# All operand tiles lie 144 bytes further, and the third and fourth unit of a block change places

## The chip, the cores and the metric

The kernel runs on one core of a Trainium2 chip. The metric is the device time of one execution in microseconds (us). A run of the kernel is repeated; the time given is the median of the runs.

## The reference

One inference step of a decoder trunk with one layer: a prompt of 256 tokens and 8 x 4 sample tokens, model width 2048, feed-forward width 5632, everything in float32. Around every sub-layer stands an RMS norm.

```python
x = x + 0.5 * rmsnorm(swiglu(rmsnorm(x, g[0]), ffn1_w_in, ffn1_w_out), g[1])
m, sg, sh = hybrid_mixer(rmsnorm(x, g[2]), mix_w_in, ..., mix_w_out, s_gla, s_hgrn)
x = x + rmsnorm(m, g[3])
x = x + 0.5 * rmsnorm(swiglu(rmsnorm(x, g[4]), ffn2_w_in, ffn2_w_out), g[5])
```

`swiglu(x)` is `(silu(x @ w_gate) * (x @ w_up)) @ w_out`. The mixer projects with one large weight, runs two gated linear recurrences on the heads (returning their states), and projects back. All inputs go through the same matrix products: 288 tokens (256 + 32) against every weight.

## The kernel before

**Products in three parts.** Tokens lie along the free dimension (T = 288), features along the partitions. A float32 operand is split into a high and a low part (`fp32r`), and a product is made of three: high x high, high x low, low x high. The normalised activations are split into the tile `xhl`, the hidden layer into `hid`, and each weight tile, loaded by SyncE into one of three `raw` buffers, into `wh`: ACT writes the high part (line 137), then DVE the low part (line 138). A weight tile is a *unit*: two k-tiles of 128 rows by 512 columns. `wh` has four buffers in the pool `hlp`, and two spare ones on the right of the memory (`hx`) around the borders between the sub-layers.

**Blocks.** `block` (line 626) makes 512 output columns: for each unit, for each of four pieces `f` of 128 columns, `two` issues six matmuls (line 647). They take a pair of k-tiles, odd and even, in the order

```python
six = [(0, 1, oh), (0, 1, ol), (0, 0, eh), (1, 1, oh), (0, 0, el), (1, 0, eh)]
```

where the first two numbers pick the weight part (0 high, 1 low; 1 odd, 0 even) and the third the moving part (o odd, e even; h high, l low). So a unit is 24 matmuls of the form 128x288. Blocks of the projections (`gate`, `up`, and those of the mixer and its output, `mo`) have 16 k-tiles, that is eight units. `out` blocks have two units, since each of the eleven 512-wide chunks of the hidden layer is multiplied as soon as it is there; four `out` blocks belong to a chunk, and the last two chunks are taken together (four units to a block). Some units are walked k by k instead (`byk`, lines 636 to 638).

The order of work per feed-forward is gate 0, up 0, gate 1, up 1, out 0, gate 2, up 2, out 1, and so on.

**Where a unit's operands lie.** A *line* is 16 bytes of each partition (`LINE = 4` floats). The start lines of all operands follow a plan:
- `tiles` (line 51) lays out `xhl` and `hid`: one line of lead, then odd high, even high (4 lines further modulo 16), odd low and even low (both 10 lines further modulo 16). Inside each part, four units share a block of memory, interleaved by 36 floats (9 lines). `PART` says which of the four places a unit takes. `xhl` begins at line 3476 and `hid` at line 9204; with the lead line both are at 5 modulo 16.
- A matmul reads its 288 moving columns in turns (`turns_of`): 4 floats (one line) from each of 8 places that are 36 lines apart, then the next line of each.
- `pieces` (line 120) lays out `wh`: odd high lies 390 lines (6 modulo 16) behind even high, odd low 129 (1) and even low 261 (5). Even high begins at a number of lines that `AHEAD_LINES` gives for the unit's number modulo 4. The four buffers of `hlp` are all at 8 modulo 16.

With `PART = (0, 3, 1, 2)` and `AHEAD_LINES = (7, 2, 0, 9)` the start lines modulo 16 are

| unit modulo 4 | moving, odd high | weights, even high | weights, odd high |
|---|---|---|---|
| 0 | 5 | 15 | 5 |
| 1 | 0 | 10 | 0 |
| 2 | 14 | 8 | 14 |
| 3 | 7 | 1 | 7 |

So a unit's first weights (odd high) lie at the same line modulo 16 as its first moving part. A unit's *start line* below is that of its odd high moving part. An even chunk of the hidden layer has the units 0 and 1, an odd one 2 and 3.

Of the kernel before, what the change touches and what calls it, by code (L numbers as in the profile page):

```python
# [9 lines left out]
F32 = mybir.dt.float32  # L10
F32R = mybir.dt.float32r
# [5 lines left out]
P = 128  # L17
TP = 256
TS = 32
T = TP + TS  # L20
# [13 lines left out]
LINE = 4  # L34
PLACES = 8
ODD_HIGH, ODD_LOW, EVEN_LOW = 1536 + 6 * LINE, 512 + LINE, 1024 + 5 * LINE
PART = (0, 3, 1, 2)
AHEAD_LINES = (7, 2, 0, 9)


def columns(t):
# [9 lines left out]
def tiles(pool, n, name):  # L51

    q = n // 2 * T
    t = pool.tile([P, LINE + 10 * LINE + 4 * q], F32R, name=name, tag=name, bufs=1)
    hs, ls = [None] * n, [None] * n
    for dst, odd, at in ((hs, 1, 0), (hs, 0, q + 4 * LINE), (ls, 1, 2 * q + 10 * LINE), (ls, 0, 3 * q + 10 * LINE)):
        r = t[:, LINE + at:LINE + at + q].rearrange("p (b g j c) -> p b g j c", g=PLACES, j=4, c=T // PLACES)
        for u in range(n // 2):
            dst[2 * u + odd] = r[:, u // 4, :, PART[u % 4], :]
    return hs, ls  # L60
# [6 lines left out]
def apart(t, step):  # L67

    return bass.AP(t.tensor, t.offset, [list(t.ap[0]), [step, 2], list(t.ap[1])])


class Weights:
# [14 lines left out]
    def add(self, src, k):  # L87
        self.srcs.append(src)
        self.at.append(LINE * AHEAD_LINES[k // 2 % 4])

# [29 lines left out]
    def pieces(self, n):  # L120

        i = self.split
        raw = self.raws.pop(i)
        pool = self.extra if i in self.extra_units else self.hlp
        hl = pool.tile([P, 2112], F32R, name=f"wh{i}", tag="wh")
        at = self.at[i]
        low = hl[:, at + ODD_LOW:at + ODD_LOW + 2 * (EVEN_LOW - ODD_LOW)]
        l = low.rearrange("p (a c) -> p a c", a=2)[:, ::-1, 0:512]
        h = apart(hl[:, at:at + 512], ODD_HIGH)
        self.parts[i] = (h, l)  # L130
        self.split += 1
        raw = raw.rearrange("p (a b) -> p a b", b=512)
        for j in range(n):
            a = slice(0, 2) if n == 1 else slice(2 * j // n, 2 * j // n + 1)
            w = min(512, 1024 // n)
            c = slice(j * w % 512, j * w % 512 + w)
            i1 = self.nc.scalar.activation(h[:, a, c], raw[:, a, c], AF.Copy).ins  # L137
            i2 = self.nc.vector.tensor_tensor(l[:, a, c], raw[:, a, c], h[:, a, c].bitcast(F32), op=ALU.subtract).ins  # L138
            self.recent = i1, i2
            yield i1, i2  # L140
# [27 lines left out]
def trunk_kernel(ctx, tc, x_prompt, x_sample, state_gla, state_hgrn, norm_gains, f1_in, f1_out, f2_in, f2_out,  # L168
# [6 lines left out]
    xpool = ctx.enter_context(tc.tile_pool(name="xpool", bufs=1))  # L175
# [69 lines left out]
    def wider(n):  # L245

        return {i for i in range(n - 44, n + 4) if i // 2 % 3 == (n + 2) // 2 % 3}
# [38 lines left out]
    x = [xpool.tile([P, T], F32, name=f"x{k}") for k in range(KT)]  # L286
    yg = [xpool.tile([P, 4, T], F32, name=f"y{k}") for k in range(4)]
    y = [yg[k // 4][:, k % 4, :] for k in range(KT)]
    xh, xl = tiles(xpool, KT, "xhl")
    rt = xpool.tile([P, T], F32, name="rt")  # L290
    rp = xpool.tile([P, T], F32, name="rp")
# [224 lines left out]
    class PreNorm:  # L516
# [3 lines left out]
        def __init__(self, name, update, ahead, at):  # L520

            self.name, self.update, self.ahead, self.at, self.late = name, update, ahead, at, []
            self.tmps = None
# [25 lines left out]
    class Fill:  # L549
# [3 lines left out]
        def __init__(self, pool, name, gains, gnext, some, ahead):  # L553
            self.gnext, self.name, self.some, self.ahead = gnext, name, some, ahead
            pool.tile([P, 8], F32, name=f"{name}gap")

            both = list(zip(*tiles(pool, 2 * EARLY, f"{name}hl")))
            self.tiles = [both[:EARLY], both[EARLY:]]
            self.gains = pool.tile([P, 32], F32, name=f"{name}g")[:, 0:EARLY]
            V.tensor_tensor(self.gains, gains[:, 0:EARLY], prm[:, gnext * KT:gnext * KT + EARLY], op=ALU.mult)  # L560
# [146 lines left out]
    def ffn(tag, gcol, gnext, pn, before, fill=None):  # L707
# [2 lines left out]
        border = []  # L710
        with ExitStack() as pools:
            fp = pools.enter_context(tc.tile_pool(name=f"ffn{tag}", bufs=2))
            fp.tile([P, 32], F32, name=f"gap_f{tag}", bufs=1)
            hid, final_tiles = {}, []
            hidden = tiles(fp, 8, f"hid{tag}")

            def do_in(c):
# [1007 lines left out]
    class Border:  # L1725


        def __init__(self, n, gains, gnext, some, ahead=0):
            self.pools = ExitStack()
            top = self.pools.enter_context(tc.tile_pool(name=f"top{gnext}", bufs=1, side="right"))  # L1730
            top.tile([P, 88], F32, name=f"gap{gnext}")
            W.begin_extra(self.pools.enter_context(tc.tile_pool(name=f"hx{gnext}", bufs=2, side="right")), wider(n))
            self.fill = Fill(self.pools.enter_context(tc.tile_pool(name=f"fl{gnext}", bufs=1, side="right")),
                             f"fill{gnext}", gains, gnext, some, ahead)

    pn = pre1 = PreNorm("pre1", x_first, FIRST, 11)
    pn.late.append(prm2)
    u, border = ffn(1, lambda k: hg1[:, k:k + 1], 2, pn, first)
    u, border = mixer(PreNorm("pre2", u, UPDATED, 11), border)
    ffn(2, lambda k: hg1[:, KT + k:KT + k + 1], None, PreNorm("pre3", u, UPDATED, 11), border.pools, border.fill)  # L1740


# [39 lines left out]
```

## Time and profile before

| | |
|---|---|
| median of 3 runs | 2148.63 us (2147.24 to 2149.55) |
| the profiled execution | 2147.9 us |
| its span, first to last instruction | 2146.1 us |
| granted TensorE clock | 0.999 |
| feed-forward 1, mixer, feed-forward 2 end at about | 804, 1360, 2146 us |
| read from HBM | 363.75 MB, 175 GB/s over the span |

How to read it. The span is what the trace holds; the run's time has 1.8 us around it. PE is TensorE's matmuls and PEld its weight loads, which overlap them; DVE is VectorE, ACT ScalarE, POOL GpSimd, SP SyncE. Matmuls are pipelined, and one's duration in the profile (some 286 ns) is longer than the time until the next one starts (some 125 ns). The *chain* follows the work that ended last back through the program; asked in order of time it gives the start of a piece, its length, and the number of instructions that were merged into it (`x192`). In a stretch in which TensorE alone sets the pace, a piece of the chain is the time that so many matmuls take, one after the other; the view can be asked for a short stretch, so that a piece is one unit (`x24`).

### The profile page before, as it was taken

Reading aid. Unit: us, or ns where it says so; the run is one execution under the profiler, and the core shown is the slowest. Engines: PE = TensorE matmul, PEld = TensorE weight load, DVE = VectorE, ACT = ScalarE, POOL = GpSimd, SP = SyncE. Lnnn points to the kernel's source line nnn. Section 1 sums busy time; section 2 is a strip of 40 time slices with the busy share of each in tenths; the row PEclk is TensorE's granted clock in tenths of the full one; section 3 lists DMA queues with packets and bytes.
Section 4 is the critical chain, followed back from the end, with each engine's and each line's share of the span. In section 5 each row is a group of like instructions: output and inputs, shape, how many; then the busy total and the mean of one; then the engine's idle time right before and its main releaser. Section 6 shows DMA issues by size and latency. Waiting matters only on the chain.

```text
span 2146.1 us, 43224 instructions
## 1 busy us (share of the span) xinstructions
PE 2134.7 (99%) x17828; PEld 2115.5 (99%) x17828; DVE 1379.6 (64%) x2253; ACT 1016.8 (47%) x1537; POOL 180.5 (8%) x327
## 2 busy tenths in 40 slices
PE   9999999999999999999999999999999999999998
PEld 9999999999999999999999999999999999999998
DVE  7655546655665568888888755854665466556656
ACT  6453433343344445655676654644334333433344
POOL 2000000000000001333110000000000020122005
PEclk9999999999999999999999999999999999999999
DMA  7665555555556654678666664555555565666556
GB/s 222 180 177 176 171 176 176 176 171 177 175 176 188 179 175 139 199 211 221 178 188 183 184 190 145 161 176 176 176 177 172 175 186 177 183 186 186 176 171 163
DMA packets 227334, 384.87 MB, mean 179 GB/s; under 512 B 21362, under 2 KB 60864, under 8 KB 227136
## 3 DMA queue, kind: packets, MB, share of 16 engines
q1 hardware_dynamic: 213872, 365.02, 56.7%
q0 software_dynamic: 10992, 16.77, 3.0%
q8 instruction: 140, 2.29, 0.4%
q10 hardware_dynamic: 2272, 0.31, 0.1%
q14 instruction: 58, 0.48, 0.1%
HBM read 363.75 MB, written 11.80 MB: 175 GB/s over the span
## 4 chain that ended last, share of the span: by engine, by line
PE 93%; DVE 3%; ACT 2%; issue 1%; DMA 1%; POOL 0%; DVEq 0%; ACTq 0%; POOLq 0%
PE gate L647 26%; PE out L647 24%; PE up L647 24%; PE hfq L647 5%; PE mo L647 4%; PE hi L647 2%; PE v L647 2%; ACT wh L137 1%; DVE wh L138 1%; PE gate L637 1%; PE gate L636 0%; PE gate L638 0%; PE os L1401 0%; PE sc L1147 0%; ACT ls L202 0%
## 5 line engine op out<-in xcount | busy, mean ns | idle before, releaser
L138 DVE TENSOR_TENSOR wh<-raw,wh 128x1024 fp32r<-128x1024 f32 (+1 forms) x676 | 821.4, 1216 | 572.2 <-ACT wh L137 571.2
L137 ACT ACTIVATE wh<-raw 128x1024 fp32r<-128x1024 f32 (+1 forms) x676 | 709.9, 1052 | 886.5 <-PE gate L647 275.9
L647 PE MATMUL gate<-xhl,wh 128*128 128x288 f32 x4584 | 588.3, 288 | 1.2 <-DVE u L740 0.8
L647 PEld LDWEIGHTS gate<-xhl,wh 128*128 128x128 f32 x4584 | 582.0, 187 | 2.8 <-issue 0.7
L647 PE MATMUL out<-hid,wh 128*128 128x288 f32 x4224 | 532.5, 286 | 0.0
L647 PEld LDWEIGHTS out<-hid,wh 128*128 128x128 f32 x4224 | 530.2, 187 | 0.1
L647 PE MATMUL up<-xhl,wh 128*128 128x288 f32 x4152 | 527.9, 287 | 0.0
L647 PEld LDWEIGHTS up<-xhl,wh 128*128 128x128 f32 x4152 | 525.3, 187 | 0.0
L831 DVE TENSOR_TENSOR y<-out,y 128x288 f32<-128x288 f32 x287 | 116.8, 451 | 73.2 <-PE out L647 73.1
L647 PE MATMUL hfq<-xhl,wh 128*128 128x288 f32 x768 | 103.3, 290 | 0.0
L647 PEld LDWEIGHTS hfq<-xhl,wh 128*128 128x128 f32 x768 | 98.6, 187 | 0.9
L788 POOL DMA_DIRECT2D xT<-b x64 | 37.2, 587 | 733.2 <-PE gate L647 550.6
L647 PE MATMUL mo<-xhl,wh 128*128 128x288 f32 x768 | 97.6, 288 | 0.2 <-ACT y L1715 0.2
L647 PEld LDWEIGHTS mo<-xhl,wh 128*128 128x128 f32 x768 | 97.1, 187 | 0.5 <-ACT y L1715 0.4
L991 POOL MEMSET ahl<- 128x512 f32 x1 | 0.5, 525 | 782.6 <-PE out L647 782.6
L742 ACT ACTIVATE hid<-u 128x288 fp32r<-128x288 f32 x88 | 37.5, 445 | 59.5 <-DVE u L741 58.0
L740 DVE TENSOR_TENSOR u<-up,rt 128x288 f32<-128x288 f32 x88 | 37.8, 451 | 29.2 <-PE up L647 29.2
L647 PE MATMUL hi<-xhl,wh 128*128 128x288 f32 x384 | 53.5, 291 | 0.0
L735 DVE TENSOR_TENSOR g<-gate,rt 128x288 f32<-128x288 f32 x80 | 33.6, 454 | 30.7 <-PE gate L647 30.7
L647 PEld LDWEIGHTS hi<-xhl,wh 128*128 128x128 f32 x384 | 50.2, 188 | 0.5
L647 PE MATMUL v<-xhl,wh 128*128 128x288 f32 x360 | 49.4, 290 | 0.0
L202 ACT ACTIVATE g<-g 128x288 f32<-128x288 f32 x88 | 36.0, 436 | 25.6 <-DVE g L735 25.2
(409 smaller groups left out, 1525.3 us busy)
## 6 DMA issues: line engine op xcount, KB each, us to landing
raw<-in_ffn_w_in_dram SPq DMA_DIRECT2D x350, 512.0 KB, 3.8
raw<-in_ffn_w_out_dram SPq DMA_DIRECT2D x176, 512.0 KB, 3.7
raw<-in_mix_w_in_dram SPq DMA_DIRECT2D x64, 512.0 KB, 4.4
raw<-in_mix_w_in_dram SPq DMA_DIRECT2D x96, 256.0 KB, 3.4
raw<-in_mix_w_out_dram SPq DMA_DIRECT2D x32, 512.0 KB, 3.8
out_dram<-s POOLq DMA_DIRECT2D x32, 256.0 KB, 3.0
s<-in_state_gla_dram SPq DMA_DIRECT2D x16, 256.0 KB, 6.3
s<-in_state_hgrn_dram SPq DMA_DIRECT2D x16, 256.0 KB, 5.8
```

Of the source, the lines that this page charges most:

```text
L137: i1 = self.nc.scalar.activation(h[:, a, c], raw[:, a, c], AF.Copy).ins
L138: i2 = self.nc.vector.tensor_tensor(l[:, a, c], raw[:, a, c], h[:, a, c].bitcast(F32), op=ALU.subtract).ins
L202: ins = S.activation(out, in_, func, **kw).ins
L637: yield lambda: PE.matmul(dst, w[0][:, a, c], parts[1], start=False, stop=False)
L647: product[0] = PE.matmul(dst, w[low][:, a, c], part, start=k == n == 0, stop=k == nk - 2 and n == 5).ins
L735: V.tensor_tensor(g, ps, rt, op=ALU.mult)
L740: ins = V.tensor_tensor(u, ps, rt, op=ALU.mult).ins
L742: S.activation(hh[f], columns(u), AF.Copy)
L788: queues[n % len(queues)].dma_start(dst[q * TS:(q + 1) * TS, 4 * g:4 * g + 4, :, cols].rearrange("p k t c -> p (k t) c"), b32[rows, q])
L831: V.tensor_tensor(y[k], ps, y[k], op=ALU.add)
L991: G.memset(ahl[:, 512:].bitcast(F32), 0.0)
```

## The change

No instruction is added, removed or moved: on every engine the instructions stand in the same order with the same waits. Addresses alone change.

```diff
-PART = (0, 3, 1, 2)
-AHEAD_LINES = (7, 2, 0, 9)
+PART = (0, 3, 2, 1)
+AHEAD_LINES = (7, 2, 9, 0)
...
 def tiles(pool, n, name):
...
-    t = pool.tile([P, LINE + 10 * LINE + 4 * q], F32R, name=name, tag=name, bufs=1)
+    t = pool.tile([P, 10 * LINE + 4 * q], F32R, name=name, tag=name, bufs=1)
...
-        r = t[:, LINE + at:LINE + at + q].rearrange("p (b g j c) -> p b g j c", g=PLACES, j=4, c=T // PLACES)
+        r = t[:, at:at + q].rearrange("p (b g j c) -> p b g j c", g=PLACES, j=4, c=T // PLACES)
...
-        at = self.at[i]
+        at = LINE + self.at[i]
...
+    xpool.tile([P, 40], F32, name="gap_x")
     xh, xl = tiles(xpool, KT, "xhl")
...
-            fp.tile([P, 32], F32, name=f"gap_f{tag}", bufs=1)
+            fp.tile([P, 40], F32, name=f"gap_f{tag}", bufs=1)
...
-            top.tile([P, 88], F32, name=f"gap{gnext}")
+            top.tile([P, 120], F32, name=f"gap{gnext}")
```

Two things happen.

Everything that TensorE reads in these products moves by 144 bytes, which is nine lines. For `xhl` a gap of 160 bytes stands ahead of the tile and the lead line of 16 bytes is gone. All that is allocated behind it (`raw`, `wh`, the pools of the sub-layers) moves by 128 bytes; inside `wh` one line is put ahead, and `hid` gets 32 more bytes of gap in exchange for its lead line. On the right side of the memory, which is filled from the end, the spare weight buffers and the fill's operands move by 112 bytes the other way (seven lines), which is the same modulo 16 lines. `raw`, read by ACT and DVE alone, moves by 128 bytes.

The third and fourth unit of each four change places, in the moving operand (`PART`) and in the weights (`AHEAD_LINES`) alike. Together the start lines modulo 16 become:

| unit modulo 4 | moving, odd high | weights, even high | weights, odd high |
|---|---|---|---|
| 0 | 14 | 8 | 14 |
| 1 | 9 | 3 | 9 |
| 2 | 0 | 10 | 0 |
| 3 | 7 | 1 | 7 |

The fourth unit stays where it was: nine lines on by the shift, nine back by the exchange.

## The prediction

> **What bounds the kernel now.** I read the page first, for what is full:
>
> ```profile
> span 2146.1 us, 43224 instructions
> PE 2134.7 (99%) x17828; PEld 2115.5 (99%) x17828; DVE 1379.6 (64%) x2253; ACT 1016.8 (47%) x1537; POOL 180.5 (8%) x327
> ...
> PE 93%; DVE 3%; ACT 2%; issue 1%; DMA 1%; POOL 0%; DVEq 0%; ACTq 0%; POOLq 0%
> ```
>
> TensorE is in action for 99% of the span and carries 93% of the chain that ended last. Nobody feeds it late: the longest waits of PE by the waits view are
>
> ```profile
> PE o L1394 <- ACT kd L1502: 1.2, 1, 1.2
> ...
> PE gate L647 <- DVE u L740: 0.8, 2, 0.5
> ```
>
> so the time is the number of matmuls times what one takes. The change adds and removes no instruction; only what one matmul takes can move the time. A busy share of 99% does not tell that, so I read the chain in order of time, where whole blocks stand as one piece:
>
> ```profile
> 302.96 24.21 PE up L647 x192
> 327.17 24.03 PE out L647 x192
> ...
> 399.63 23.98 PE out L647 x192
> ```
>
> 192 matmuls of one form, 128x288, take 24.21 us in an `up` block (126.1 ns each) and 23.98 us in four `out` blocks (124.9 ns). Something in the `up` block costs 0.23 us. The same view, asked for one unit of 24 matmuls at a time, finds where. Units 0 to 3 of this `up` block, then unit 4:
>
> ```profile
> 302.96 2.99 PE up L647 x24
> 305.96 2.99 PE up L647 x24
> 308.95 3.08 PE up L647 x24
> 312.03 3.04 PE up L647 x24
> 315.07 2.99 PE up L647 x24
> ```
>
> The third and fourth unit of each four are slow, by 0.09 and 0.05 us. That could be the lines at which they start (14 and 7), the jump by which they are reached, or merely their number in the block, through what ACT and DVE do beside them. The `out` blocks, of two units each, tell these apart. First an odd chunk, whose units start at lines 14, 7, 14, 7:
>
> ```profile
> 327.17 2.99 PE out L647 x24
> 330.16 3.02 PE out L647 x24
> 333.18 2.99 PE out L647 x24
> 336.17 3.02 PE out L647 x24
> ```
>
> Here a unit at line 14 costs 2.99 us: the line alone isn't slow. Now the last, double chunk, lines 14, 7, 5, 0, 14, 7, from its first unit and from its fifth:
>
> ```profile
> 762.02 2.99 PE out L647 x24
> ...
> 774.01 3.08 PE out L647 x24
> 777.10 3.04 PE out L647 x24
> ```
>
> The same line 14 costs 2.99 us when the unit before it lay at line 7 (762.02) and 3.08 us when it lay at line 0 (774.01, though this is the first unit of its block). So neither the number nor the line decides, but **the pair of a unit and the one before it**. At such a seam TensorE still streams the last product of the old unit, from its even high part (start line + 4), while it already loads the new unit's first weights, which lie at the new unit's own start line modulo 16. I call old line + 4 - new line, modulo 16, the distance of the seam. Inside a unit, from one 128-column piece to the next, it is always 4. An even chunk gives the seams 0 to 5 and 5 to 0:
>
> ```profile
> 399.63 2.99 PE out L647 x24
> 402.62 2.99 PE out L647 x24
> 405.61 3.01 PE out L647 x24
> ```
>
> All seams of the kernel before, with the time of the unit that follows:
> - distance 9 (5 to 0): 2.99 us
> - distance 13 (7 to 14): 2.99 us
> - distance 15 (0 to 5): 3.01 us
> - distance 11 (14 to 7): 3.02 us, and 3.04 us where the unit at 14 was slow itself
> - distance 6: 3.08 us for 0 to 14, but 2.99 us for 7 to 5 (the rows at 302.96 and 315.07)
>
> **The change part by part.**
>
> *All operands 9 lines (144 bytes) further.* Moving parts and weights go together, so within every unit each product meets its weights at the same difference as before. The rows above have units of 2.99 us at the lines 5, 0 and 14, so the lines as such have no price, and I put the common shift at 0 us. What covers it is that both shifts are equal, and that isn't quite so: the two spare weight buffers on the right move 7 lines down, which is the same modulo 16 but not modulo 32. They hold 24 of the 626 units that are walked in this form. If each of these became as slow as the slowest row, that would be 24 x 0.09 = 2.2 us; I take 0, and keep 2.2 for the range.
>
> *Third and fourth unit change places.* The start lines become 14, 9, 0, 7. The seams of a block of eight units were 9, 6, 11, 6; they become 9 (14 to 9), 13 (9 to 0), 13 (0 to 7), 13 (7 to 14). Both distances have rows of 2.99 us for the unit behind them. Four units take now, by the row of 192 at 302.96, 24.21 / 2 = 12.105 us; they will take 4 x 2.99 = 11.96 us: 0.145 us less. In the built program there are 118 places where a unit at line 14 follows one at 0 (112 in the blocks of eight units, 6 in the two double chunks; where a unit is walked k by k, it isn't counted and keeps its time). 118 x 0.145 = 17.1 us.
>
> In the `out` blocks nothing is gained: even chunks go from 5, 0 to 14, 9 with distances 9 and 15 as before; odd chunks from 14, 7 to 0, 7, so that distance 11 (now 7 to 0, 3.02 us) is at the first unit and 13 (0 to 7, 2.99 us) at the second: 0 us.
>
> *What is late next.* Per unit ACT and DVE split one weight tile:
>
> ```profile
> L138 DVE TENSOR_TENSOR wh<-raw,wh 128x1024 fp32r<-128x1024 f32 (+1 forms) x676 | 821.4, 1216 | 572.2 <-ACT wh L137 571.2
> L137 ACT ACTIVATE wh<-raw 128x1024 fp32r<-128x1024 f32 (+1 forms) x676 | 709.9, 1052 | 886.5 <-PE gate L647 275.9
> ```
>
> One after the other they are 1.05 + 1.22 = 2.27 us, below 2.99 us, and run a unit or more ahead. They read `raw`, which moves by 128 bytes, and write parts that move by 144; the profile prices no such shift. The nearest rows are two operations of ACT on one form:
>
> ```profile
> L742 ACT ACTIVATE hid<-u 128x288 fp32r<-128x288 f32 x88 | 37.5, 445 | 59.5 <-DVE u L741 58.0
> ...
> L202 ACT ACTIVATE g<-g 128x288 f32<-128x288 f32 x88 | 36.0, 436 | 25.6 <-DVE g L735 25.2
> ```
>
> They differ by 2%; that much on 2.27 us is 0.05 us either way, inside the 0.7 us that is free. The cover is thin only in the mixer, as two stretches show (columns: PE, PEld, DVE, ACT, POOL, clock, DMA share, GB/s):
>
> ```profile
> 302.96:327.17 24.21, 24.21 (x195) 24.21 (x194) 11.31 (x13) 9.48 (x12) 0.00 (x0) 1.00 0.55 175
> 1100.00:1200.00 100.00, 99.90 (x1121) 96.94 (x1120) 89.43 (x202) 71.37 (x160) 7.58 (x11) 1.00 0.63 181
> ```
>
> DVE is at 11.3 of 24.2 us in the `up` block, but at 89% here. 25 of the 118 places lie in the mixer's projections, worth 3.6 us; I let a third of that be lost to DVE, 1.2 us (between nothing and all of it). The weights come at 175 GB/s and would need 177; the row above shows 181.
>
> **Sum.** 2147.9 us of the profiled execution (span 2146.1, 1.8 us around it) - 17.1 + 1.2 = **2132 us**. The median of the runs, 2148.63, lies 0.7 us higher; I don't add this.
>
> *A rule that speaks against it.* "SBUF — State Buffer" of the Trainium skill, section "Who interferes with whom", says that PE and ACT never wait on anyone, and "TensorE: Matmul & The Clock Gate", section "Step-by-step: what each phase is for", that loading the next weights takes no read bandwidth from the running matmul. By these the place of operands would be worth nothing and the time 2148 us. The trace doesn't agree: the same form on the same line takes 2.99 or 3.08 us per 24.
>
> **The rivals.**
> - *One of the new seams is worse than its distance says.* Distance 6 shows that it doesn't tell all: 7 to 5 is harmless, 0 to 14 isn't. Distance 13 is measured for one pair only, 7 to 14; 9 to 0 and 0 to 7 are carried over. One unit in four left at 3.04 us gives 118 x (0.145 - 0.05) = 11 us, 2137 us; at 3.08 us 118 x (0.145 - 0.09) = 6.5 us, 2141 us. Chance 0.12.
> - *The change does nothing*: the slowness belongs to something that moves along, so that another two of the four units are slow. Then 12.105 us stay and the time is 2148 us. For it: nobody in the trace names what a slow matmul waits for. Against: the four seams of distance 13 in each odd `out` chunk. Chance 0.08, which includes the skill's rule.
> - *Slower: both carried-over seams start a slow stretch.* The unit at 0 and the one at 7 then cost 3.08 us each: 2.99 + 2.99 + 3.08 + 3.08 = 12.14 us, 118 x 0.035 = 4.1 us more; in the odd chunks of `out` a pair goes from 6.01 to 3.02 + 3.08 = 6.10 us, 36 times 0.09 = 3.2 us. Together 2155 us, and 2161 us if the unit at 14 after a slow one still takes 3.04 us (118 x 0.05). It is slower from the point where two of the three new seams are slow. For it: after 0 to 14 the slowness lasts into a second unit, so it can feed itself. Against: distance 6 stood at all slow starts, and vanishes. Chance 0.08.
>
> **How the numbers follow.** The forecast has 0.72, between 2128 us (nothing lost in the mixer, also the 3.01 and 3.02 us of `out` gone, 30 x 0.02 + 36 x 0.03 = 1.7 us, and a run 0.7 us below the profiled one, as the lowest shown is) and 2137 us (all of the mixer's 3.6 us lost and the 2.2 us of the spare buffers paid). With the first rival, up to 2142 us, that is 0.84; a little of it falls outside. Range 2128 to 2143 us. 0.2%, about what a measurement of this kernel can tell from no change, is 4.3 us: faster 0.84, same 0.08, slower 0.08.
>
> **What would show it.** Right: the `up` and `gate` blocks at 23.92 us (8 x 2.99), all their units at 2.99 us, `out` blocks at 23.98 and 24.03 us as now. The step on seams is wrong if a unit of 3.04 us or more remains in the steady blocks; which line it has tells which seam. The step on the common shift is wrong if the second unit (9 after 14, distance and differences as before) leaves 2.99 us, or if the means of L137 and L138 move by more than 2%. The mixer's loss is wrong if its `hfq` and `hi` blocks shorten as much as `gate` does.

## The result, and the profile after

The changed kernel takes 2138.11 us (median of 4 runs, 2137.37 to 2138.94), the kernel before beside it 2149.09 us (4 runs, 2147.24 to 2149.63). The ratio is 0.995, with a 95% interval of 0.9934 to 0.9966: faster by about 11 us. Between the two profiled executions the gain is 9.2 us (2147.9 to 2138.67 us). The forecast was 2132 us, 15.9 us below the profiled execution. So direction and range hold, and of the expected gain about four tenths are missing between the profiled executions, about a third between the medians. The time lies in the band that the forecast gave to its first rival (2137 to 2142 us), not in its own (2128 to 2137 us).

The page of the changed kernel, with the rows that answer to those of before:

```profile
span 2136.9 us, 43224 instructions
PE 2122.5 (99%) x17828; PEld 2103.1 (98%) x17828; DVE 1378.8 (65%) x2253; ACT 1016.0 (48%) x1537; POOL 180.4 (8%) x327
...
L138 DVE TENSOR_TENSOR wh<-raw,wh 128x1024 fp32r<-128x1024 f32 (+1 forms) x676 | 821.4, 1216 | 568.4 <-ACT wh L137 567.4
L137 ACT ACTIVATE wh<-raw 128x1024 fp32r<-128x1024 f32 (+1 forms) x676 | 709.2, 1051 | 880.0 <-PE gate L648 269.1
```

The same instructions, TensorE still full for 99% of a span that is 9.2 us shorter, and the two splits of the weights at the same duration (1216 ns, and 1051 after 1052 ns). So what has moved is mainly what one matmul takes. From line 289 on, all program lines stand one higher after the change: line 647 is now 648.

The chain in order of time, at the blocks that were shown of before:

```profile
277.59 24.01 PE gate L648 x192
301.60 23.95 PE up L648 x192
325.54 24.19 PE out L648 x192
349.73 23.95 PE gate L648 x192
...
397.62 23.93 PE out L648 x192
```

`up` fell from 24.21 to 23.95 us; 23.92 was forecast. The `out` blocks of an even chunk (397.62) went from 23.98 to 23.93, but those of an odd chunk (325.54) rose from 24.03 to 24.19, where no change was forecast. Cut into units, the four of the `up` block at 301.60 and the second of the odd `out` chunk:

```profile
301.60 2.99 PE up L648 x24
304.58 2.99 PE up L648 x24
307.57 2.99 PE up L648 x24
310.56 3.01 PE up L648 x24
...
328.55 3.04 PE out L648 x24
```

The third unit's 3.08 us are gone. What is left of slowness sits in the unit at line 7 that follows line 0: 3.01 us here, 3.04 us in `out`. In a `gate` block behind an even chunk (277.59) the third unit, which follows line 9 as in `up`, takes 3.01 and not 2.99 us, and the fourth 3.04 us: the same pairs at the same lines cost more there, so the pair alone doesn't set the time in this kernel either.

Where the 9.2 us came from, in both profiled executions from the start of each stretch to the start of the next (after minus before, us, rounded):

| stretch | forecast | measured |
|---|---|---|
| `gate` and `up` of both feed-forwards (80 places) | -11.6 | -10.2 |
| `out`, steady chunks | 0 | +0.8 |
| `out` of chunk 8 in feed-forward 1 | 0 | +1.1 |
| the two double `out` chunks (6 places) | -0.9 | -0.8 |
| mixer with its start (25 places) | -2.4 | -0.2 |
| `mo` (7 places) | -1.0 | -0.5 |
| start of the program, and what else stands before chunk 1 | 0 | +0.5 |
| end of the program, behind the last `out` block | 0 | +0.2 |
| sum | -15.9 | -9.2 |

The row on the end of the program hides two larger differences that cancel. In the kernel before the granted clock from 2135 us on is 0.81, and the small matmuls there take 1.7 us longer than in the changed kernel; but in the changed kernel the time from TensorE's last matmul to the end of the span is 1.8 us longer. Nothing in the change accounts for either.

The +1.1 us of chunk 8 is a wait of which the kernel before had only 0.2 us (24.19 us for this chunk, 23.98 us for the other even ones). The chain there, with its longer pieces:

```profile
673.00 3.58 DMA raw<-in_ffn_w_out_dram
...
677.70 1.24 DVE wh L138
...
678.95 5.18 DMA raw<-in_ffn_w_out_dram
...
684.24 1.07 ACT wh L137
...
685.33 1.23 DVE wh L138
686.56 0.37 DVE u L742
...
693.34 17.48 PE out L648 x138
```

Two loads of `raw` (3.58 and 5.18 us) stand in the chain, then the splits that wait for them, then the elementwise work of VectorE that is queued behind the second split. The windows of 685 to 700 us show what TensorE loses there (columns: stretch, PE, PEld, DVE, ACT, POOL, clock, DMA share, GB/s), after and before:

```profile
685.00:700.00 15.00, 14.23 (x112) 13.79 (x111) 12.90 (x24) 7.07 (x10) 0.00 (x0) 1.00 0.65 193
```

```profile
685.00:700.00 15.00, 15.00 (x120) 14.87 (x119) 12.98 (x24) 7.84 (x10) 0.00 (x0) 1.00 0.65 199
```

112 matmuls in place of 120, with the clock at 1.00 in both.

### The profile page after: what moved, and what is told of

It is laid out like the page before. It is cut to its first block, busy times and chain, and to the rows that moved or that the text cites. A ratio compares the mean times of both kernels' runs of the same rounds, so it can differ in the third digit from the quotient of the medians.

```text
span 2136.9 us, 43224 instructions
## 1 busy us (share of the span) xinstructions
PE 2122.5 (99%) x17828; PEld 2103.1 (98%) x17828; DVE 1378.8 (65%) x2253; ACT 1016.0 (48%) x1537; POOL 180.4 (8%) x327
## 4 chain that ended last, share of the span: by engine, by line
PE 93%; DVE 3%; ACT 2%; DMA 1%; issue 1%; SPq 0%; ACTq 0%; DVEq 0%
PE gate L648 26%; PE out L648 24%; PE up L648 23%; PE hfq L648 5%; PE mo L648 3%; PE hi L648 2%; PE v L648 2%; DVE wh L138 1%; ACT wh L137 1%; PE gate L638 1%; PE gate L637 1%; PE gate L639 1%; PE qk L648 1%; DMA raw<-in_mix_w_out_dram 0%; DMA raw<-in_ffn_w_out_dram 0%
## 5 line engine op out<-in xcount | busy, mean ns | idle before, releaser
L138 DVE TENSOR_TENSOR wh<-raw,wh 128x1024 fp32r<-128x1024 f32 (+1 forms) x676 | 821.4, 1216 | 568.4 <-ACT wh L137 567.4
L137 ACT ACTIVATE wh<-raw 128x1024 fp32r<-128x1024 f32 (+1 forms) x676 | 709.2, 1051 | 880.0 <-PE gate L648 269.1
L648 PE MATMUL up<-xhl,wh 128*128 128x288 f32 x4152 | 522.5, 286 | 0.0
L648 PEld LDWEIGHTS up<-xhl,wh 128*128 128x128 f32 x4152 | 519.8, 187 | 0.0
```

The lines of the kernel that those rows point to most:

```text
L648: product[0] = PE.matmul(dst, w[low][:, a, c], part, start=k == n == 0, stop=k == nk - 2 and n == 5).ins
```

## The experiments

Two questions stood open. What makes the unit slow: the seam's distance, as forecast (theory **S**), or something else that the change also moved? And why is part of the gain missing? All ratios below are against runs of the kernel before on the same chip, with the 95% interval in brackets.

### Each half of the change alone

The shift without the exchange: `PART` and `AHEAD_LINES` keep their old order, the rest is the change. The start lines are 14, 9, 7, 0, and every distance is that of before: 9, 6, 11, 6.

```diff
-PART = (0, 3, 2, 1)
-AHEAD_LINES = (7, 2, 9, 0)
+PART = (0, 3, 1, 2)
+AHEAD_LINES = (7, 2, 0, 9)
```

> All operands nine lines further, the units in their old order: start lines 14, 9, 7, 0, seams at distance 9, 6, 11, 6 as in the kernel before. Theory S (only the distance of a seam counts, a common shift is free): an up block takes 24.21 us with its third unit at 3.08 us, and the time is that of before, 2148 us. Rival L (the lines at which units start count too): the units' times differ from before; if the shift brings the whole gain, 2138 us and 23.95 us for an up block.

The exchange without the shift: only these two lines are changed in the kernel before. The start lines are 5, 0, 7, 14.

```diff
-PART = (0, 3, 1, 2)
-AHEAD_LINES = (7, 2, 0, 9)
+PART = (0, 3, 2, 1)
+AHEAD_LINES = (7, 2, 9, 0)
```

> Third and fourth unit exchanged, nothing shifted: start lines 5, 0, 7, 14, seams at distance 9, 13, 13, 13 as after the change. S: an up block takes 23.95 us, the third unit is the one that stays at 3.01 us or more (it follows a unit 7 lines lower, as the fourth does in the changed kernel), and the time is 2138 us. L: other times for the units; 2148 us if the order brings nothing by itself.

Measured: the shift alone 2139.36 us, ratio 0.9962 [0.9947, 0.9977]; the exchange alone 2138.35 us, 0.9956 [0.9941, 0.9971]. Either half brings nearly the whole gain, and both together no more than one, within the intervals. The chain of the kernel with the shift alone, whole blocks and then units of its `up` block:

```profile
276.89 23.98 PE gate L648 x192
300.86 23.97 PE up L648 x192
324.83 24.19 PE out L648 x192
```

```profile
300.86 2.99 PE up L648 x24
303.86 2.99 PE up L648 x24
...
309.84 3.01 PE up L648 x24
```

And of the kernel with the exchange alone:

```profile
300.94 23.99 PE up L647 x192
324.93 24.03 PE out L647 x192
```

In the `up` block of the second, the first and the third unit take 3.01 us each and the other two 2.99 us, and its odd `out` chunks stay at 24.03 us.

The first run fells S. All four distances are as before, the harmful 6 among them twice, and the block takes 23.97 us. It even has the pair of lines 0 to 14 (fourth unit to the next first one), which before took 128.4 ns a matmul from start to start; here it takes 124.8. The formula had fitted every row of before and told the wrong thing: it named the place where the slowness begins, not what makes it.

### The shift in steps

If not the distance, then the absolute place. Four kernels only change gaps: the changed kernel 8 and 16 lines further, and the kernel before 2 and 4 lines further (on the right of the memory as far the other way or along, so that all operands keep together).

```diff
-    xpool.tile([P, 40], F32, name="gap_x")
+    xpool.tile([P, 72], F32, name="gap_x")
...
-            top.tile([P, 120], F32, name=f"gap{gnext}")
+            top.tile([P, 152], F32, name=f"gap{gnext}")
```

> The changed kernel with all operands a further 8 lines on: start lines 6, 1, 8, 15, seams at distance 9, 13, 13, 13. S: 23.95 us for an up block and 2138 us as after the change. L with a period of 16 lines: other times for some units, so an up block off by 0.05 us or more; L with a period of 8 lines: as S.

The second has 104 and 184 in place of 72 and 152.

> The changed kernel with all operands a further 16 lines on: the same start lines modulo 16. S and L both expect the changed kernel's times, 23.95 us for an up block and 2138 us. A third theory, that lines count modulo 32 or more, expects other units' times.

```diff
+    xpool.tile([P, 8], F32, name="gap_x")
...
-            top.tile([P, 88], F32, name=f"gap{gnext}")
+            top.tile([P, 80], F32, name=f"gap{gnext}")
```

> The kernel before with all operands 2 lines further: start lines 7, 2, 0, 9, seams as before at distance 9, 6, 11, 6. Shifting by 9 lines alone ended the slow third unit, shifting by 8 or 16 changed nothing. If lines count with a period of two: as before, 24.21 us for an up block, third unit 3.08 us, 2148 us. If with a period of four or eight: the third unit may fall to 2.99 us, 23.97 us for an up block, 2139 us.

The fourth has 16 and 72 in place of 8 and 80.

> The kernel before with all operands 4 lines further: start lines 9, 4, 2, 11, seams as before. Period of two or four lines: as before, 24.21 us for an up block and 2148 us. Period of eight: the third unit may fall to 2.99 us, 23.97 us for an up block, 2139 us.

Measured: the changed kernel 8 lines further 2138.08 us, 0.9956 [0.9941, 0.9971], 16 lines further 2137.94 us, 0.9957 [0.9941, 0.9974]; the kernel before 2 lines further 2148.59 us, 1.0001 [0.9991, 1.001], 4 lines further 2146.01 us, 0.9993 [0.9983, 1.0002]. The last two in the chain:

```profile
302.05 24.21 PE up L648 x192
```

```profile
303.01 24.21 PE up L648 x192
```

The even shifts tried change nothing: 24.21 us as before for 2 and 4 lines, and no unit's time for 8 and 16 lines on top of the nine. What is left is an odd number (theory P: odd or even line decides). One line, the smallest step, with the old order of units (start lines 6, 1, 15, 8):

```diff
+    xpool.tile([P, 8], F32, name="gap_x")
...
-    t = pool.tile([P, LINE + 10 * LINE + 4 * q], F32R, name=name, tag=name, bufs=1)
+    t = pool.tile([P, 10 * LINE + 4 * q], F32R, name=name, tag=name, bufs=1)
...
-        at = self.at[i]
+        at = LINE + self.at[i]
...
-            fp.tile([P, 32], F32, name=f"gap_f{tag}", bufs=1)
+            fp.tile([P, 40], F32, name=f"gap_f{tag}", bufs=1)
```

(The lead line in front of `at` in `tiles` goes too, as in the change.)

> The kernel before with all operands one line (16 bytes) further, units in their old order: start lines 6, 1, 15, 8. Shifts by 2, 4, 8 and 16 lines changed no unit's time and the shift by 9 did. Theory P (whether a unit starts at an odd or an even line is all that counts of a common shift): as with 9 lines, 23.97 us for an up block, third unit 2.99 to 3.00 us, 2139 us. Rival: the 9 lines did something else, and one line leaves 24.21 us and 2148 us.

Measured: 2139.19 us, 0.9962 [0.9948, 0.9975].

```profile
301.29 23.97 PE up L648 x192
325.26 24.19 PE out L648 x192
```

Both rows are those of the nine-line shift, within 0.01 us. Sixteen bytes more in front of everything end the slow stretch; 32 and 64 bytes don't. So of the common shifts tried, the odd ones (1 and 9 lines) end the slow stretch and the even ones (2 and 4) don't. An odd shift isn't the only way, since the exchange alone ends it too, without any shift.

### What keeps the slow unit slow

In the kernel before, the times from one matmul's start to the next in the third unit repeat after twelve, which is two pieces of six; a fast unit repeats after six (ns, means over 38 steady `gate` and `up` blocks):

```
fast unit   125.0 123.3 124.2 124.2 124.2 125.8
third unit  125.8 123.4 124.2 125.8 129.2 126.6 | 133.4 134.1 129.2 129.1 129.2 130.0
```

That is 124.45 ns against 128.33 ns on average, for the same six products. In the fourth unit the first nine matmuls are slow (124 to 134 ns), then it is fast without anything between. One theory (M) is that this is a second rhythm, which goes on once it has begun; the rival is that each product of that unit is slow by its own place. A small matmul (128x32, of ones) between the second and third piece of the third unit tells them apart. It writes into columns of the accumulator that nobody reads.

```diff
             for f in range(nf):
+                if f == 2 and u % 4 == 2:
+                    PE.matmul(ps[0][:, T:T + 32], onesR, onesR[:, 0:32], start=False, stop=True, skip_group_check=True)
                 two(w, f, u * per)
```

> The kernel before with one small matmul more (128x32, on a constant, into columns that nobody reads) in the middle of each third unit, between its second and third piece. Theory M (the seam starts a slow stretch that then keeps itself going): behind the small matmul the third unit runs at 124.5 ns per matmul, so its second half takes 1.49 us instead of 1.53 us, and the fourth unit takes 3.02 us instead of 3.04 us. Rival A (each product of this unit is slow by where its operands lie): the second half stays at 1.53 us and the fourth unit at 3.04 us.

The same small matmul ahead of the third unit (`f == 0`) separates the old unit's last product from the new unit's first weights. If the overlap at the seam starts the slowness, the unit behind it is fast.

> The kernel before with the same small matmul ahead of each third unit, at the seam from line 0 to line 14. Theory M: the slow stretch isn't started, the third unit takes 2.99 to 3.02 us beside what the small matmul costs (some 0.06 to 0.12 us), and the fourth 3.02 us. Rival A: 3.08 us beside it, and 3.04 us for the fourth.

Measured, one run each: 2154.97 us with the small matmul inside the unit, 2160.59 us with it ahead. The chain of the first, from the `up` block's start:

```profile
303.18 7.53 PE up L647 x60
310.71 0.02 PE up L661
310.73 1.48 PE up L647 x11
312.20 3.02 PE up L647 x24
```

The small matmul itself and the disturbance behind it cost some 0.13 us (27.5 ns, then 215 and 135 ns to the next two starts). Behind these the third unit runs in the fast rhythm to its end, at the same places that were slow before, and the fourth unit takes 3.02 us in place of 3.04. So M holds here: the places of the second half aren't slow by themselves.

The chain of the second:

```profile
304.09 5.98 PE up L647 x48
310.07 0.01 PE up L661
310.09 12.20 PE up L647 x96
```

Here the third unit has the slow rhythm from its second matmul on, number for number, though another matmul lies between it and the old unit: its first weights start to load 128 ns after the start of the old unit's last product, in place of 2 to 3 ns. M had expected a fast unit here, so that part of it is wrong. The overlap at the seam, by which the forecast explained the pair, isn't needed to start the slowness. If the neighbour at the seam doesn't matter, perhaps the moment does at which the unit begins (theory T). A matmul of 96 columns in the same place moves the unit's start by 18 ns (45.0 in place of 26.7 ns from the small matmul's start to the next):

```diff
-                    PE.matmul(ps[0][:, T:T + 32], onesR, onesR[:, 0:32], start=False, stop=True, skip_group_check=True)
+                    PE.matmul(ps[0][:, T:T + 96], onesR, onesR[:, 0:96], start=False, stop=True, skip_group_check=True)
```

> The kernel before with a small matmul of 96 columns, in place of 32, ahead of each third unit. With 32 columns the third unit stayed slow although its first weights were no longer loaded beside the last product of the unit before. Theory T (the moment at which the unit is entered decides which of two rhythms it takes): another length may leave the third unit at 2.99 us behind its first matmul. Rival (this unit goes slow whenever it is entered in another way than from line 7): 3.08 us behind the small matmul as with 32 columns.

Measured, one run: 2154.08 us, 6.5 us less than with 32 columns, though each small matmul takes longer.

```profile
303.32 5.98 PE up L647 x48
309.30 0.05 PE up L661
309.34 12.11 PE up L647 x96
```

Four units behind it take 12.11 us in place of 12.20. From start to start, the third unit of both (ns, first two pieces of four):

```
32 columns  210.1 123.3 124.3 125.7 129.3 126.6 | 133.4 134.1 129.2 129.1 129.2 129.9
96 columns  195.8 135.8 129.1 130.0 125.0 125.9 | 125.0 123.4 124.2 124.1 124.2 125.8
```

Behind 96 columns the same unit, at the same line, after the same unit, falls into the fast rhythm after five matmuls and stays there. So a unit at this place can run in both rhythms, and the way in which it is entered decides. Whether that is the moment alone (T) is not shown, since the length of the inserted matmul changed with it. The fourth unit still takes 3.04 us here, with nine slow matmuls at its start, though the third ended in the fast rhythm; so these nine aren't simply the third unit's rhythm carried on.

### The wait at chunk 8

At chunk 8 of the first feed-forward the two spare buffers come into use: `wider(n)` opens them 44 units ahead of the border, so that the loads may run two units further ahead, and for a short time more loads are wanted than come. If this is the wait of 1.1 us (theory W), it should move or go when the spares open later.

```diff
-        return {i for i in range(n - 44, n + 4) if i // 2 % 3 == (n + 2) // 2 % 3}
+        return {i for i in range(n - 36, n + 4) if i // 2 % 3 == (n + 2) // 2 % 3}
```

> The changed kernel with the two spare weight buffers in use from 36 units ahead of a border instead of 44. In the changed kernel the first out blocks of chunk 8, where the spares come into use, take 25.3 us instead of 23.93 us, and the chain runs there through late weight loads and DVE. Theory W (the spares call for two more units at once, DVE's splits wait for their loads, and the evacuations queue behind them): chunk 8 falls to 24.0 us or less, the wait moves to where the spares now start or goes, and the time falls by up to 2 us, 2136 to 2138 us. Rival D (the loads are late there whatever the spares do): chunk 8 stays at 25 us, 2138 us.

The second has 28 in place of 36.

> The changed kernel with the spare buffers in use from 28 units ahead of a border. W: chunk 8 at 24.0 us or less, 2136 to 2138 us. D: chunk 8 at 25 us, 2138 us.

Measured: with 36 units 2137.98 us, 0.9956 [0.9941, 0.997]; with 28 units 2137.89 us, 0.9954 [0.9939, 0.9969]. The four `out` blocks of chunk 8 took 25.27 us in the changed kernel. With 36 units they take 24.96 us, where W had expected 24.0 us or less; by the order of the units the spares then still open inside this chunk, which holds the 40th to the 33rd unit ahead of the border. With 28 units:

```profile
684.64 23.93 PE out L648 x192
```

With the opening behind the chunk the wait is gone, so it hangs on where the spares open. How much of it comes from TensorE's being earlier is not shown: the same chunk takes 24.33 and 24.68 us in the two kernels that keep the slow unit (2 and 4 lines further), 24.63 us with the shift alone and 25.28 us with the exchange alone.

But the time is not lower: the span is 2137.2 us (2136.9 with 44 units). Besides the 1.3 us of chunk 8 this execution gained 0.9 us in its first blocks, where the program is the same. It lost 0.5 us in the mixer, 0.5 us in `mo` and 1.5 us behind the last `out` block, where the granted clock from 2125 to 2130 us is 0.50 (1.00 with 44 units) and the chain runs through POOL. Whether the late opening causes any of these losses is not shown. No version tried beats the changed kernel by what can be measured.

## Why the prediction was right or wrong

**TensorE sets the time, by what one matmul takes.** Right: same instructions, same busy share, and against the 9.2 us net, `gate` and `up` gave 10.2.

**The pair of a unit and the one before it decides, through the seam's distance.** Right for every row of before, wrong as a cause. The shift alone keeps all distances and ends the slowness (23.97 us); the small matmul of 32 columns takes the overlap away and does not end it. Shown instead: a stretch of matmuls can run in a slow rhythm (128.33 ns) or in a fast one (124.45 ns); in the third unit the slow one goes on until a small matmul breaks it; whether the unit gets into it depends on odd or even lines (1 and 9 lines further against 0, 2 and 4), on the unit before, and on the way of entry (32 or 96 columns ahead). That the total fell into the range is therefore luck as far as the mechanism goes: the exchange alone brings the gain, as the step said, but so does the shift, which it put at nothing. What inside TensorE or its memory makes the two rhythms stays open. No view names it.

**The common shift costs and brings 0 us.** Wrong in kind, and hidden in the sum, since the exchange brings the same. The sign that was named for it, a second unit off 2.99 us, did not show (2.99 us), because it asked only whether a shift costs. Alone the shift makes the kernel faster, 0.9962 [0.9947, 0.9977]. The step argued that lines have no price because units at several lines were fast. It did not ask what a step does to the slow pair, which in the trace of before stood at one set of lines only.

**118 places by 0.145 us.** In the feed-forwards the term was too large by one seam, in the main. In `up`, the units at the new seams 14 to 9, 9 to 0 and 7 to 14 came out as forecast (2.99 us). The seam 0 to 7, carried over from 7 to 14 because both have distance 13, costs 3.01 us there, and 3.04 us for the fourth unit of a `gate` block behind an even chunk. In rows: `up` fell by 0.26 us and not 0.29, `gate` behind an even chunk by 0.22 (24.23 to 24.01); over the 80 places of both feed-forwards that is 10.2 us and not 11.6. This is the first rival, in most blocks at less than half of its price (0.02 us a unit, where it had 0.05 or 0.09). The larger part of the missing gain lies elsewhere: 2.2 us in the mixer and 1.9 us in `out`.

**`out` blocks 0 us.** Wrong by that same seam: 0 to 7 stands four times in each odd chunk and takes 3.04 us there, so that such a chunk pays 24.19 and not 24.03 us. Even chunks gained 0.05 us. Over both feed-forwards +0.8 us.

**ACT and DVE stay hidden.** Right for their durations (L137 and L138 moved by 0.1% at most), wrong for one place: at chunk 8 the spare buffers open, and the loads that they call for are late. The loads, not the engines, were late, and VectorE's queue handed the delay on: +1.1 us. That it grew because TensorE now comes earlier fits, but isn't shown.

**Mixer: 3.6 us, a third lost to DVE.** Wrong, and for another reason. Of the mixer's `hfq` blocks the page says before, and after:

```profile
L647 PE MATMUL hfq<-xhl,wh 128*128 128x288 f32 x768 | 103.3, 290 | 0.0
```

```profile
L648 PE MATMUL hfq<-xhl,wh 128*128 128x288 f32 x768 | 103.4, 290 | 0.0
```

Nothing was gained, so nothing was lost to DVE. In before the third unit of each four in `hfq` took 126.4 ns a matmul on average, not 128.4: the places had been counted, but their times had not been read. Of these eight units only three ran in the slow rhythm. Small matmuls of the scans stand between the pieces there, and in one of the three the slow rhythm ends behind such a matmul, after twelve products. That the others stay fast for the same reason fits, but was not tried.

**`mo` 1.0 us.** Came out at half, 0.5 us less. The long stretch of matmuls in it, before and after, became shorter by 0.6 us:

```profile
1257.38 71.50 PE mo L647 x564
```

```profile
1253.66 70.88 PE mo L648 x564
```

Ahead of this stretch TensorE waits for ACT, in the chain of after behind late loads, and this wait varies: with all operands 2 lines further the stretch takes 71.50 us as before, and `mo` 1.5 us more. (With the shift alone the stretch takes 72.55 us, with a granted clock of 0.90 from 1253 to 1270 us.) So this term isn't settled to better than that.

**The rule that speaks against it.** "SBUF — State Buffer" of the Trainium skill, section "Who interferes with whom", says that PE never waits on anyone. What the forecast derived from it, that the place of operands is worth nothing, doesn't hold here: 16 bytes in front of all operands move the `up` block from 24.21 to 23.97 us, with the same instructions and the granted clock at 0.999 and 1.0. Whether a slow matmul waits on another engine, no run shows.

## What to carry to other kernels

Where one instruction form has two durations, ask first whether the slow one comes in stretches: look at the times from start to start in order, and put something small in the middle of a stretch. A formula that fits all rows of one kernel is not a cause; move everything by the smallest step with all differences kept, which here, in one run, would have shown that the distance isn't the cause. And count only those places for a gain at which the trace shows the slowness itself: 25 of the 118, in the mixer, gave 0.2 us together.

## What the runs showed of the hardware

- In this program 192 matmuls of 128x288 take 24.21 us, or 23.97 us when all operands stand 16 bytes further; 32 and 64 bytes further change nothing (24.21).
- Two rhythms of the same six products, 124.45 and 128.33 ns on average. The slow one has a period of twelve matmuls, twice that of the program's pattern, and in the third unit it lasted to the end unless a small matmul stood in between; in the fourth unit the matmuls are fast after nine.
- A matmul of 32 columns ahead of the unit leaves the slow rhythm in place, one of 96 columns in the same spot prevents it, and the longer one makes the kernel 6.5 us faster than the shorter (2154.08 and 2160.59 us, one run each; 24.31 and 24.43 us for an `up` block).
- A lone small matmul costs far more than its columns: 27.5 ns to the next start for 32 columns, but 215 and 135 ns for the two matmuls behind it, so that it adds about 0.13 us to the 250 ns of these two.
